# Three Q loads of a cross-covariance attention kernel issued in two parts of 68 + 60, 104 + 24 and 120 + 8 partitions

## The chip, the cores and the metric

One core of one Trainium2 chip. The metric is the time of one execution on the device in microseconds. "Before" and "after" are medians of runs. A ratio is the mean time of one kernel's fast runs over that of the other kernel's fast runs of the same rounds on the same chip, so it is not quite the ratio of the medians quoted beside it; its 95% interval stands with it. A difference in us beside a ratio is the ratio less one, times the median of before of those rounds.

The profile is that of one execution. In its lines PE is TensorE, PEld its weight loads, DVE is VectorE, ACT ScalarE, POOL GpSimd and SP SyncE; a q marks an engine's sequencer. Besides the page, the argument uses two kinds of record in the trace: the semaphore updates that the DMA engines write when their share of a transfer has landed (1552 before, 16 for each of 97 transfers), and the DMA packets, each with start, duration and size, but without the number of its engine.

## The reference

```python
Q_norm = Q / (np.linalg.norm(Q, axis=-2, keepdims=True) + 1e-10)   # Q, K, V: (8, 12, 512, 64) float32
K_norm = K / (np.linalg.norm(K, axis=-2, keepdims=True) + 1e-10)
attn = np.einsum('bhnd,bhne->bhde', Q_norm, K_norm)                # 64 x 64 for each head
attn = softmax(attn)                                               # shortened
return np.einsum('bhnd,bhde->bhne', V, attn)
```

## The kernel before

The 96 heads are 24 units of 4 heads. Each unit has three loads (Q, K, V) of 128 partitions by 4 KB, and there are 25 stores. All transfers are issued by SyncE on one queue; a planner in the kernel fixes the order of all pieces of work. At most eight transfers are in flight, as a transfer waits for the landing of the one eight places before it (in the profile, issues stand 1.27 us apart and the median from issue to landing is 10.1 us, eight times that).

```python
NB = dict(qk=6, v=5, vb=4, qkb=3, vt=3, so=10, sm=2, ab=3)       # buffers
...
def load_qk(u, x):
    if x == 0:
        qk32[u] = qp.tile([128, 2, T, D], F32, name="qk32")        # T = 16, D = 64: 4 KB for Q, 4 KB for K
    nc.sync.dma_start(out=qk32[u][:, x], in_=(Qu, Ku)[x][u * 128:(u + 1) * 128])

def store(s, i, k=None):
    rows = slice(None) if k is None else slice(k * (J // 2), (k + 1) * (J // 2))
    o = Of[s, i].rearrange("p r (j d) -> p r j d", d=D)
    nc.sync.dma_start(out=o[:, :, rows], in_=so[s, i][:, :, rows])
...
piece(("lq", u), {"DMA": X}, free, [back("lk", u, 1)], at, load_qk, u, 0)
piece(("lk", u), {"DMA": X}, free, [("lq", u)], at, load_qk, u, 1)
```

## Time and profile before

| | before |
|---|---|
| time | 132.25 us (131.68 to 132.82, 2 runs) |
| span of the profiled run | 129.8 us |
| moved | 50.66 MB, 390 GB/s over the span, 400 to 420 in the steady part |
| DMA packets under 512 B | 1552 = 97 transfers x 16 |
| 4 KB load packets | 9216, of 159 ns nearly all |

The lines behind it stand in the prediction. In the row "GB/s" each number is one of 40 slices of the span. Here the stream runs at its limit and shows as a flat row (400 to 420), so a hole in it is lost time. The row of digits above it ("DMA") tells less, as will be seen.

### The profile page before, as it was taken

What the parts mean: (1) busy time and instruction counts of PE and PEld (TensorE: products, weight loads), DVE (VectorE), ACT (ScalarE), POOL (GpSimd) and SP (SyncE); (2) the same over time, 40 slices, a digit from 0 to 9 for tenths busy, and PEclk for the clock granted to TensorE, in tenths of its full rate; (3) what the DMA queues carried; (4) which work ended last, traced back from release to release, by engine and by line L of the source; (5) the groups of instructions that cost most, each with busy time, mean ns of one, the idle gap of its engine ahead of it and who ended that gap; (6) DMA issues with size and microseconds to landing.
All of it is one profiled execution on the core that took longest, in us unless ns stands there. A gap on an engine that the chain in (4) does not pass through costs nothing.

```text
span 129.8 us, 4986 instructions
## 1 busy us (share of the span) xinstructions
PE 81.7 (63%) x2160; PEld 67.1 (52%) x2160; DVE 96.2 (74%) x161; ACT 75.2 (58%) x179; POOL 56.2 (43%) x49
## 2 busy tenths in 40 slices
PE   0045392985829835959578999479596555857610
PEld 0045381863628624749455777268374443747410
DVE  2445979999899697698999774969876778489500
ACT  0000509569566562375768569949889823795830
POOL 3000664815985308029490393371483534275000
PEclk9999999599965775556985559955999965797555
DMA  4999999999999999999999999999999999999892
GB/s 136 375 399 421 408 414 404 409 413 403 410 405 407 405 408 414 402 415 415 409 419 403 415 412 414 413 417 407 416 407 414 413 412 407 409 402 403 346 334 81
DMA packets 17190, 50.66 MB, mean 390 GB/s; under 512 B 1552, under 2 KB 2064, under 8 KB 17168
## 3 DMA queue, kind: packets, MB, share of 16 engines
q1 hardware_dynamic: 17168, 50.34, 98.1%
q8 instruction: 17, 0.28, 0.8%
q14 instruction: 5, 0.04, 0.1%
HBM read 37.75 MB, written 12.58 MB: 388 GB/s over the span
## 4 chain that ended last, share of the span: by engine, by line
DVE 34%; PE 28%; POOL 10%; ACT 9%; issue 7%; DMA 5%; SPq 1%; POOLq 0%; ACTq 0%; DVEq 0%
PE gram L196 14%; POOL r L219 9%; DVE kqs L223 8%; DVE scr L203 7%; DVE qkb L178 7%; PE po L280 6%; PE vps L265 5%; DMA qk<-in_K_dram 5%; DVE n L215 4%; DVE ab L251 4%; ACT so L154 3%; ACT vt L154 3%; PE lg L236 3%; DVE vt L156 2%; ACT ex L242 2%
## 5 line engine op out<-in xcount | busy, mean ns | idle before, releaser
L196 PE MATMUL gram<-qkb 32*128 32x128 bf16 x1536 | 37.5, 270 | 15.5 <-DVE qkb L178 10.1
L196 PEld LDWEIGHTS <-qkb 32*128 32x128 bf16 x1536 | 32.6, 121 | 19.4 <-DVE qkb L178 15.5
L158 POOL TENSOR_SCALAR vb<-v 128x1024 bf16<-128x1024 f32 x24 | 28.0, 1167 | 31.6 <-DMA v<-in_V_dram 29.0
L178 DVE CAST qkb<-qk 128x1024 bf16<-128x1024 f32 x48 | 33.2, 718 | 6.9 <-DMA qk<-in_Q_dram 5.1
L219 POOL TENSOR_TENSOR r<-n,mhalf 128x8 f32<-128x8 f32 x12 | 23.1, 1924 | 29.6 <-DVE n L215 17.3
L280 PE MATMUL po<-ab,vt 128*64 128x128 bf16 x384 | 21.5, 254 | 20.5 <-ACT vt L154 12.8
L154 ACT COPY so<-po 128x512 f32<-128x512 f32 x47 | 26.4, 591 | 11.3 <-PE po L280 11.0
L154 ACT COPY vt<-vps 128x1024 bf16<-128x1024 bf16 (+1 forms) x23 | 27.7, 1218 | 2.0 <-PE vps L265 1.8
L280 PEld LDWEIGHTS <-vt 128*64 128x64 bf16 x384 | 15.0, 127 | 26.0 <-ACT vt L154 15.4
L242 ACT ACTIVATE ex<-lg,rq 128x64 f32<-128x64 f32 x48 | 14.4, 314 | 20.9 <-PE lg L236 18.0
L203 DVE SCALAR_TENSOR_TENSOR scr<-gram,eye 64x512 f32<-64x512 f32 x24 | 16.5, 689 | 7.0 <-PE gram L196 6.7
L265 PE MATMUL vps<-identb,vb 128*128 128x128 bf16 x192 | 19.1, 262 | 0.7 <-ACT kq L154 0.7
L265 PEld LDWEIGHTS <-vb 128*128 128x128 bf16 x192 | 14.5, 118 | 3.4 <-issue 2.1
L223 DVE TENSOR_TENSOR kqs<-kq,r 64x512 f32<-64x512 f32 x8 | 11.1, 1386 | 3.7 <-POOL r L219 3.5
L251 DVE TENSOR_TENSOR ab<-ex,rinv 64x256 bf16<-64x256 f32 x24 | 10.9, 453 | 0.7
L236 PE MATMUL lg<-eye,kqs 64*128 64x64 f32 x48 | 7.0, 284 | 5.5 <-DVE kqs L223 5.1
L242 ACT ACTIVATION_READ_ACCUMULATOR ex<-lg,rq 128x1 f32 x48 | 9.8, 205 | 0.0
L236 PEld LDWEIGHTS lg<-eye,kqs 64*128 64x128 f32 x48 | 5.0, 177 | 7.8 <-DVE kqs L223 6.4
L154 ACT ACT_TABLE_LOAD x1 | 1.3, 1283 | 13.3 <-DVE scr L203 13.3
L215 DVE TENSOR_REDUCE n<-scr 128x8 f32<-128x512 f32 x12 | 8.2, 684 | 0.4
L154 ACT COPY kq<-gram 64x512 f32<-64x512 f32 x12 | 7.0, 580 | 2.0 <-DVE scr L203 1.7
L230 DVE COPY rq<-r 64x4 f32<-64x4 f32 x12 | 4.9, 411 | 2.3 <-POOL r L219 2.0
(15 smaller groups left out, 18.5 us busy)
## 6 DMA issues: line engine op xcount, KB each, us to landing
qk<-in_Q_dram SPq DMA_DIRECT2D x24, 512.0 KB, 10.1
qk<-in_K_dram SPq DMA_DIRECT2D x24, 512.0 KB, 10.2
v<-in_V_dram SPq DMA_DIRECT2D x24, 512.0 KB, 10.1
out_dram<-so SPq DMA_DIRECT2D x23, 512.0 KB, 10.0
out_dram<-so SPq DMA_DIRECT2D x2, 256.0 KB, 4.3
```

The source lines that it names most:

```text
L154: nc.scalar.copy(o, i)
L158: nc.gpsimd.tensor_scalar(out=o, in0=i, scalar1=1.0, scalar2=0.0, op0=ALU.mult, op1=ALU.add)
L178: nc.vector.tensor_copy(qkb[u][:, :, x * D:(x + 1) * D], qk32[u][:, x])
L196: nc.tensor.matmul(gram[s][:, h, r, 0], x, x, start=(t == 0), stop=(t == T - 1))
L203: nc.vector.scalar_tensor_tensor(out=scr[s][half], in0=gram[s][half, :, :, 0, half].rearrange("p h r d -> p (h r) d"), scalar=1e-20, in1=e ...
L219: nc.gpsimd.tensor_tensor(out=r8[s], in0=n2[s], in1=mhalf, op=ALU.pow)
L223: (nc.vector if eng == "DVE" else nc.gpsimd).tensor_tensor(out=kqs[s][HI], in0=kq[s][HI], in1=r8[s][HI, :, None].to_broadcast([D, 2 * HU, ...
L236: nc.tensor.transpose(l[:, h, :], kqs[s][HI, 2 * h:2 * h + 2].rearrange("p r d -> p (r d)"), eye2[HI])
L242: nc.scalar.activation(e[:, h, :], lg[s][:, h, :], AF.Exp, scale=rq[s][:, h:h + 1], accum_out=z[:, h:h + 1])
L251: nc.vector.tensor_tensor(out=a[half, :, half], in0=e[half], in1=ri[half, :, None].to_broadcast([D, HU, D]), op=ALU.mult,)
L265: nc.tensor.transpose(ps[:, n, j, :], vb[s][:, t].rearrange("p r d -> p (r d)"), identb)
L280: nc.tensor.matmul(po[s, x][e * D:(e + 1) * D, j].rearrange("p r d -> p (r d)"), w, ab[s][:, h, :])
```

## The change

The intent is to learn which engines carry a transfer that has not 128 rows. Nothing else is touched; the result stays correct.

```diff
+    CUTS = {(15, 0): 68, (18, 0): 104, (21, 0): 120}
...
-        nc.sync.dma_start(out=qk32[u][:, x], in_=(Qu, Ku)[x][u * 128:(u + 1) * 128])
+        cut = CUTS.get((u, x), 128)
+        for p0, p1 in ((0, cut), (cut, 128)):
+            if p1 > p0:
+                nc.sync.dma_start(out=qk32[u][p0:p1, x], in_=(Qu, Ku)[x][u * 128 + p0:u * 128 + p1])
```

## The prediction

In it, k is the number of engines that carry a part. Parts of 68, 60, 104, 24, 120 and 8 rows are taken to run on 4, 15, 13, 12, 15 and 8 engines; the profile after has as many semaphore updates for each. "Engines 0 to 3" is only a name for the four of the 68 rows. Its +16 rows can be worked out from these counts: with even rows, an engine that is in both parts of each cut gets 17 + 4, 8 + 2 and 8 + 1 rows in place of three times 8, so 13, 2 and 1 more. That the rows are even and that the same four engines are in all six parts is the author's estimate, as are the chances of the cases (a) to (c).

> **What bounds the kernel now.** I read the page from the top: busy times, the 40 slices, the DMA queues, then the chain that ended last, and after it SyncE's own waits and its issues in order of time, and the idle times of the second half. The page:
>
> ```profile
> span 129.8 us, 4986 instructions
> PE 81.7 (63%) x2160; PEld 67.1 (52%) x2160; DVE 96.2 (74%) x161; ACT 75.2 (58%) x179; POOL 56.2 (43%) x49
> ...
> DMA  4999999999999999999999999999999999999892
> GB/s 136 375 399 421 408 414 404 409 413 403 410 405 407 405 408 414 402 415 415 409 419 403 415 412 414 413 417 407 416 407 414 413 412 407 409 402 403 346 334 81
> DMA packets 17190, 50.66 MB, mean 390 GB/s; under 512 B 1552, under 2 KB 2064, under 8 KB 17168
> ...
> q1 hardware_dynamic: 17168, 50.34, 98.1%
> q8 instruction: 17, 0.28, 0.8%
> ...
> DVE 34%; PE 28%; POOL 10%; ACT 9%; issue 7%; DMA 5%; SPq 1%; POOLq 0%; ACTq 0%; DVEq 0%
> ```
>
> No compute engine is above 74%, while the 16 DMA engines are busy in every slice but the first and the last few and move a flat 400 to 420 GB/s. The chain gives DMA only 5% because it is followed back through DVE, PE and POOL; it does not say that the DMA has slack. The 1552 packets under 512 B are 97 transfers times 16: each transfer writes one small completion packet on every engine, so today each runs on all 16.
>
> SyncE's waits from 55 us on, and a stretch of its issues:
>
> ```profile
> SPq L173 <- ACT so L154: 10.4, 10, 2.3
> SPq L173 <- DMA out_dram<-so: 7.1, 8, 0.9
> SPq L164 <- DMA qk<-in_K_dram: 6.8, 8, 1.0
> SPq L168 <- DMA v<-in_V_dram: 6.6, 6, 2.2
> SPq L164 <- DMA qk<-in_Q_dram: 6.2, 8, 0.9
> ```
>
> ```profile
> 53.00 0.33 SPq L164 DMA_DIRECT2D qk<-in_Q_dram  x1
> 54.20 0.33 SPq L164 DMA_DIRECT2D qk<-in_K_dram  x1
> 55.49 0.40 SPq L173 DMA_DIRECT2D out_dram<-so  x1
> 56.75 0.33 SPq L168 DMA_DIRECT2D v<-in_V_dram  x1
> ```
>
> Issuing takes 0.33 us, but issues stand 1.27 us apart: before each, SyncE waits for the landing of the transfer eight places earlier. The page's median from issue to landing is 10.1 us, which is eight times 1.27. So the landings pace the kernel, and a landing is the landing of the last of 16 engines. 1.27 us for 8 rows of 4 KB on each engine is 0.159 us for a row.
>
> Landings are not even. Each completion packet's semaphore update is recorded with its time: around 63 us the 16 updates of one transfer spread over 1.9 us, around 94 us over 3.4 us, with four engines within 0.1 us of the last and the other twelve 0.9 to 3.4 us earlier. An engine loses about 1.3 us each time one of the 17 blocks of instructions (q8, 16 KB) passes over it. [...] the ninth block (69 us) sets one of the engines already late back again, so that the last update of all jumps by 1.28 us. The 17th (124.5 us) again makes one engine the straggler: in the last three stores 15 engines are done 1.1 us before it. The trace does not number the engines, so which ones carry the blocks is unknown.
>
> How close compute is behind the loads, from matching each landing with its cast: the Q load of unit 15 has 5.4 us to spare, unit 17 has 0.7, unit 20 has 0.7, unit 21 has 0.02. The waits from 60 us on agree:
>
> ```profile
> POOL r L219 <- DVE n L215: 12.8, 5, 4.0
> POOL vb L158 <- DMA v<-in_V_dram: 11.1, 7, 3.9
> ...
> DVE qkb L178 <- DMA qk<-in_Q_dram: 0.4, 1, 0.4
> ```
>
> The reader is to see that GpSimd sits waiting for V, and that DVE hardly waits for Q: it is just fed in time.
>
> [...]
>
> **The change part by part.** The schedule is made from the same plan, so the order of work on PE, DVE, ACT and GpSimd is the same; SyncE has 102 rows for 99. Three more issues of 0.33 us are 1.0 us of an engine that waits most of the time: no cost. The lanes of the eight-deep issue window shift by one, two, three: with a split inside it, the window holds half a megabyte less of eight, so some 9 us in flight instead of 10, still well over the time that an engine needs.
>
> The cost is the rows. [...]
>
> Engines 0 to 3: +16 rows, 16 x 0.159 = 2.54 us (2.07 + 0.32 + 0.16). [...] The lost time doesn't come back: in the last store the straggler works alone and still takes 0.042 us for each 1 KB row, as the engines do when all are busy; so an engine is at its own limit and does not speed up when others idle.
>
> How much reaches the end depends on where engines 0 to 3 stand in the spread.
> (a) One of them is the straggler of the end. It is busy without a gap from the first loads to its last store, so the end moves by all of it: +2.5 us. Compute allows that: Q of unit 21 lands 2.5 us later against 0.02 of slack, and [...] its K cast and all after it move by about 1.9 us (0.6 us of an existing wait for POOL is used up). The last issue moves from 124.6 to 126.5 us, within what a 2.5 us later DMA end needs.
> (b) They contain block-carrying engines, but not that one. These are some 1.1 us ahead at the end, so the DMA gives 2.5 - 1.1 = +1.4; the compute shift of up to 1.9 us, less what the shorter tail of the queue gives back, says about the same.
> (c) All four are among those that no block hits, 2.2 to 3.5 us ahead at the end: 0 to +0.4 us.
>
> Sum, with chances 0.45, 0.33 and 0.22: 0.45 x 2.5 + 0.33 x 1.4 + 0.22 x 0.2 = +1.6 us. [...]
>
> **The rivals.** First: k stays 16, rows dealt out unevenly (68 as 5 and 4). Then no engine gets more than a row or two extra, and the time stays at 132.2. For it: nothing but that no other row count was seen. I give it 0.13. Second: case (c), or slack absorbs it all, same time; against it, the slack of 0.02 and 0.7 us listed above, and that SyncE's issue follows landings. Third: 68 rows on 4 engines is slower than its rows, since four engines must carry 272 KB while the issue window stalls all others, so the starved engines add theirs: about +4 us. Against it: the early engines land 8 us after issue around 63 us and need under 3 (the first transfer's first update came 2.9 us after its issue), so their queues do not run dry over 2 us. Fourth: faster, because the engine relieved of 24 rows is the straggler. It helps only if engines 0 to 3 are all far ahead; hardly possible.
>
> **Range and chances.** 0.87 x 1.6 is +1.4; the most likely single case is +2.5, so I put the point a little above the mean: 132.25 + 1.65 = 133.9. The low end is no change (132.2), the high end is the full 2.5 on a baseline that itself ran from 131.68 to 132.82, plus some loss of order: 135.2. The line of 2% is 2.65 us, just beyond the full cost: same 0.80, slower 0.19, faster 0.01.
>
> **What would show it.** Small packets: 94 x 16 + 4 + 15 + 13 + 12 + 15 + 8 = 1571 under 512 B [...], 1600 if every part runs on 16. The updates of unit 15's Q load: 4 for the first part, the last of them 9 rows or 1.4 us later than the pace. After it the spread of the 16 updates grows by up to 2.1 us if engines 0 to 3 were late already, and shrinks if they were early: that also tells case (a) from (c). Busy times of the compute engines are unchanged within their scatter, and the idle time of GpSimd before its V casts and of DVE before its Q casts grows. The mean GB/s falls by 1 to 2%. The prediction is wrong if the count is 1571 and the time doesn't move (slack took it, or (c)), or if the time grows by over 3 us (idle engines, third rival).

## The result, and the profile after

139.31 us (139.08 and 139.53, 2 runs), ratio 1.0532 (1.0434 to 1.063): slower by 7.0 us. Both runs are in the fast state. The page after:

```profile
span 137.1 us, 4992 instructions
...
PE 82.1 (60%) x2160; PEld 67.2 (49%) x2160; DVE 95.7 (70%) x161; ACT 75.4 (55%) x179; POOL 56.0 (41%) x49
...
DMA  4999999999999999999999999999999999999982
GB/s 165 372 398 422 410 406 406 409 409 405 411 405 403 409 414 408 409 358 239 374 409 414 353 285 343 422 403 377 270 310 408 409 412 407 409 402 381 353 297 87
DMA packets 17209, 50.66 MB, mean 370 GB/s; under 512 B 1571, under 2 KB 2083, under 8 KB 17187
...
DMA 53%; PE 14%; DVE 12%; ACT 6%; issue 4%; POOL 3%; SPq 3%; DVEq 0%; POOLq 0%; ACTq 0%
```

The busy times of the compute engines are those of before. The bytes are the same. But "GB/s" has three holes, around slices 19, 24 and 29, down to 239, 285 and 270. The digits show none of it: they stay at 9, since a packet that is held up (in the holes 235 to 269 ns at the median, in place of 159) counts as busy. The chain of waits now gives DMA 53% in place of 5%.

The small packets are 1571, as the prediction's sum foretold (1600 would be 16 for every part), and the semaphore updates say the same: the six parts have 4, 15, 13, 12, 15 and 8 updates from engines, each with one more that comes some 0.5 us after the issue, whose source no run shows.

The same stretches of both kernels, in the view of busy time by stretch (stretch, its length, busy time of PE, PEld, DVE, ACT and POOL with instructions, granted clock, DMA share, GB/s). Before:

```profile
50.00:59.00 9.00, 5.81 (x115) 4.54 (x104) 7.19 (x13) 4.34 (x12) 2.97 (x3) 0.50 1.03 410
59.00:66.00 7.00, 5.19 (x186) 4.45 (x188) 5.99 (x12) 5.00 (x13) 5.09 (x5) 0.88 1.04 414
...
76.00:84.00 8.00, 6.20 (x174) 4.90 (x164) 5.61 (x11) 7.00 (x16) 3.38 (x4) 0.89 1.03 411
...
93.00:102.00 9.00, 5.64 (x196) 4.57 (x197) 6.84 (x13) 8.25 (x18) 4.46 (x5) 1.00 1.03 410
```

After:

```profile
50.00:59.00 9.00, 5.84 (x211) 4.87 (x213) 7.06 (x14) 5.78 (x15) 3.20 (x3) 0.88 1.03 409
59.00:66.00 7.00, 5.04 (x136) 4.18 (x128) 6.42 (x12) 4.28 (x13) 5.53 (x5) 0.75 1.05 286
...
76.00:84.00 8.00, 6.41 (x180) 5.30 (x180) 5.12 (x9) 5.52 (x14) 4.17 (x3) 0.79 1.02 306
...
93.00:102.00 9.00, 4.27 (x144) 3.31 (x136) 3.36 (x5) 6.21 (x9) 3.90 (x4) 0.99 1.04 305
```

The bytes missing in the three stretches, as time at the rate of before: 7 x (1 - 286/414) = 2.2, 8 x (1 - 306/411) = 2.0, 9 x (1 - 305/410) = 2.3 us, together 6.5 of the 7.0 us. So each cut costs about the same, though by the prediction the first gives four engines thirteen rows too many and the last gives them one. That already speaks against the prediction's sum.

The packets say how. Outside the holes a 4 KB load packet takes 159 ns in both kernels. In the holes most of them take over 200 ns: 88% of those that start between 60 and 66 us, 68% between 77 and 83, 72% between 94 and 101, with medians of 269, 235 and 251 ns. In the first hole that is some 270 packets, more than the 128 of the cut load, so other loads are among them. After the first 10 us, 34 were over 200 ns before, and 905 after. Added up over 159 ns and shared among 16 engines, the excess is 8.0 us after against 1.3 before: 6.7 us. Store packets (2 KB) hardly change, 84 ns for most in the holes too.

That the waits for loads grow is the consequence. Two compute groups, with their busy time, the mean of one, their idle time, and how much of it ended with a load; before, then after:

```profile
L158 POOL TENSOR_SCALAR vb<-v 128x1024 bf16<-128x1024 f32 x24 | 28.0, 1167 | 31.6 <-DMA v<-in_V_dram 29.0
L178 DVE CAST qkb<-qk 128x1024 bf16<-128x1024 f32 x48 | 33.2, 718 | 6.9 <-DMA qk<-in_Q_dram 5.1
```

```profile
L159 POOL TENSOR_SCALAR vb<-v 128x1024 bf16<-128x1024 f32 x24 | 28.3, 1183 | 45.3 <-DMA v<-in_V_dram 45.1
L182 DVE CAST qkb<-qk 128x1024 bf16<-128x1024 f32 x48 | 35.0, 751 | 16.5 <-DMA qk<-in_Q_dram 13.6
```

### The profile page after: what moved, and what is told of

Read it like the earlier page. It is cut to its first block, busy times and chain, and to the rows that moved or that the text cites. A ratio compares the mean times of both kernels' runs of the same rounds, so it can differ in the third digit from the quotient of the medians.

```text
span 137.1 us, 4992 instructions
## 1 busy us (share of the span) xinstructions
PE 82.1 (60%) x2160; PEld 67.2 (49%) x2160; DVE 95.7 (70%) x161; ACT 75.4 (55%) x179; POOL 56.0 (41%) x49
## 2 busy tenths in 40 slices
DMA packets 17209, 50.66 MB, mean 370 GB/s; under 512 B 1571, under 2 KB 2083, under 8 KB 17187
## 4 chain that ended last, share of the span: by engine, by line
DMA 53%; PE 14%; DVE 12%; ACT 6%; issue 4%; POOL 3%; SPq 3%; DVEq 0%; POOLq 0%; ACTq 0%
DMA out_dram<-so 29%; DMA qk<-in_K_dram 16%; DMA qk<-in_Q_dram 9%; PE gram L200 6%; PE po L284 4%; POOL r L223 3%; DVE scr L207 3%; DVE qkb L182 3%; ACT so L155 2%; SPq L168 2%; PE vps L269 2%; DVE kqs L227 2%; DVE ab L255 2%; ACT ex L246 2%; DVE n L219 2%
## 5 line engine op out<-in xcount | busy, mean ns | idle before, releaser
L200 PE MATMUL gram<-qkb 32*128 32x128 bf16 x1536 | 38.5, 273 | 22.6 <-DVE qkb L182 16.2
L182 DVE CAST qkb<-qk 128x1024 bf16<-128x1024 f32 x48 | 35.0, 751 | 16.5 <-DMA qk<-in_Q_dram 13.6
L223 POOL TENSOR_TENSOR r<-n,mhalf 128x8 f32<-128x8 f32 x12 | 22.5, 1876 | 23.6 <-DVE n L219 19.8
L284 PEld LDWEIGHTS <-vt 128*64 128x64 bf16 x384 | 15.5, 131 | 26.4 <-ACT vt L155 15.8
L269 PE MATMUL vps<-identb,vb 128*128 128x128 bf16 x192 | 18.4, 255 | 0.8 <-ACT kq L155 0.7
L269 PEld LDWEIGHTS <-vb 128*128 128x128 bf16 x192 | 13.9, 115 | 3.6 <-issue 2.0
L227 DVE TENSOR_TENSOR kqs<-kq,r 64x512 f32<-64x512 f32 x8 | 10.1, 1260 | 3.0 <-POOL r L223 2.8
L157 DVE COPY vt<-vps 128x512 bf16<-128x512 bf16 (+1 forms) x5 | 4.1, 840 | 1.3 <-PE vps L269 1.3
```

Source lines behind the costliest of these rows:

```text
L182: nc.vector.tensor_copy(qkb[u][:, :, x * D:(x + 1) * D], qk32[u][:, x])
L200: nc.tensor.matmul(gram[s][:, h, r, 0], x, x, start=(t == 0), stop=(t == T - 1))
L223: nc.gpsimd.tensor_tensor(out=r8[s], in0=n2[s], in1=mhalf, op=ALU.pow)
L227: (nc.vector if eng == "DVE" else nc.gpsimd).tensor_tensor(out=kqs[s][HI], in0=kq[s][HI], in1=r8[s][HI, :, None].to_broadcast([D, 2 * HU, ...
L269: nc.tensor.transpose(ps[:, n, j, :], vb[s][:, t].rearrange("p r d -> p (r d)"), identb)
L284: nc.tensor.matmul(po[s, x][e * D:(e + 1) * D, j].rearrange("p r d -> p (r d)"), w, ab[s][:, h, :])
```

## The experiments

The theories after the first look:

- *Rows* (the prediction): engines 0 to 3 get more rows, an engine is at its own limit, landings follow the slowest.
- *Window*: half-size transfers in the eight-deep window, or the issues themselves, starve the engines.
- *Crowded partitions* (new; in the expectations of the first round still "slow packets", without a place): engines that write certain partitions of SBUF at the same time hold each other up, and the parts bring this about. When it was set up it was a guess, from the 905 packets over 200 ns of the change; the added loads below test it.

### One cut at a time, and a cut along the other axis

Cuts alone: `CUTS` has only the named entry.

```diff
-    CUTS = {(15, 0): 68, (18, 0): 104, (21, 0): 120}
+    CUTS = {(15, 0): 68}          # only68; likewise only104, only120
```

> Only the 68 + 60 cut of unit 15. Rows theory (what the prediction said): 13 extra rows on engines 0 to 3, about +2.1 us over the kernel before. Slow-packet theory (while a transfer whose rows do not lie as those of a 128-row load is under way, every 4 KB load packet takes 240 to 330 ns in place of 159): about a third of the +7.1 us, +2.3 to +2.7 us. This run alone hardly parts them; its sisters do.

Measured: 134.07 us against 131.68, ratio 1.0152 (1.0085 to 1.0218), +2.0 us; 312 load packets over 200 ns.

> Only the 104 + 24 cut of unit 18. Rows theory: 2 extra rows, +0.3 us. Slow-packet theory: about +2.2 us, with one dip of the GB/s of some 6 us around 77 to 84 us and load packets of 240 to 330 ns in it, none elsewhere.

Measured: 134.45 against 131.68, ratio 1.0192 (1.012 to 1.0264), +2.5 us; 298 packets over 200 ns. One hole, at the 24th slice, and a flat row elsewhere up to the last five slices:

```profile
GB/s 143 388 407 424 407 408 404 412 406 413 404 406 402 407 413 412 408 415 412 418 403 415 393 243 361 412 409 417 411 413 412 419 414 407 404 380 322 284 249 168
DMA packets 17199, 50.66 MB, mean 381 GB/s; under 512 B 1561, under 2 KB 2073, under 8 KB 17177
```

> Only the 120 + 8 cut of unit 21. Rows theory: 1 extra row, +0.2 us. Slow-packet theory: about +2.4 us, with one dip of some 6 us around 95 us.

Measured: 133.59 against 131.68, ratio 1.0115 (1.0084 to 1.0145), +1.5 us; 252 packets over 200 ns. It is less than the +2.4 us expected, but some nine times the 0.16 us of one extra row. The three together make 6.0 us, the change 7.0 with an interval of 5.7 to 8.3.

The other axis:

```diff
-        nc.sync.dma_start(out=qk32[u][p0:p1, x], in_=...)
+        nc.sync.dma_start(out=qk32[u][:, x, t0:t1], in_=src[:, t0:t1])   # t 0 to 8, then 8 to 16
```

> The same three loads in two parts each, but cut along the free axis: two transfers of 128 partitions by 2 KB. Each part runs on 16 engines with 8 rows each, as any load of before. Window theory (the eight-deep issue window, taken up by half-size transfers, or the three extra issues themselves, starve the engines): about +7 us like the change. Slow-packet and rows theories: within 0.5 us of the kernel before, no dip, no long packets; 1600 packets under 512 B.

Measured: 132.58 against 131.68, ratio 1.0052 (1.0008 to 1.0095), +0.7 us, a little more than the 0.5 expected. 1600 small packets, 36 load packets over 200 ns, no hole. The same number of issues and the same window as the change cost a tenth of it: the window theory falls.

### Parts on all 16 engines, cut at other partitions; and stores

```diff
-    CUTS = {(15, 0): 68, (18, 0): 104, (21, 0): 120}
+    CUTS = {(15, 0): 112, (18, 0): 112, (21, 0): 112}     # cut64: 64 in place of 112
```

> Three Q loads cut 112 + 16. Both parts run on 16 engines (7 rows and 1 row), so every engine has its 8 rows as before[...]. Rows theory: no change beyond the +0.7 us that the column cut cost, 1600 small packets, no long ones. Slow-packet theory with the SBUF side as its place [...]: three dips, load packets of 240 to 330 ns, +4 to +7 us. If only engine counts that are no power of two are slow, no dip either.

Measured: 137.27 against 131.93, ratio 1.0398 (1.0324 to 1.0472), +5.2 us. 1600 small packets: all 16 engines carry both parts, 7 rows and 1 row each if the rows are even, and yet 754 load packets are over 200 ns. An odd number of engines is not needed for the loss, nor, with even rows, are more rows for some.

For 64 + 64, the figures of the crowding theory stand first:

> Three Q loads cut 64 + 64: 16 engines for each part, 4 rows each, rows even. [...] 4 KB packets of some 318 ns in three dips and +4 to +7 us. Rows theory: +0.7 us as the column cut.

Measured: 138.15 against 132.43, ratio 1.0481 (1.0416 to 1.0546), +6.4 us; 790 packets over 200 ns; of the load packets that start between 60 and 65 us, 75% are over 200 ns and the middle half takes 201 to 286. The row with the three holes:

```profile
GB/s 143 395 405 420 407 408 406 408 410 406 405 412 401 410 414 409 407 372 268 410 404 415 352 248 352 416 410 413 263 333 411 416 416 405 410 402 379 369 253 160
DMA packets 17238, 50.66 MB, mean 374 GB/s; under 512 B 1600, under 2 KB 2112, under 8 KB 17216
```

Now the same two parts of 64 partitions, but the even ones and the odd ones:

```diff
-        for p0, p1 in ((0, cut), (cut, 128)): ...
+        parts = [slice(0, 128, 2), slice(1, 128, 2)] if (u, x) in CUTS else [slice(0, 128)]
+        for p in parts:
+            nc.sync.dma_start(out=qk32[u][p, x], in_=src[p])
```

The crowding theory's figure is again the first:

> Three Q loads cut into even and odd partitions, 64 each: 16 engines, 4 rows each, as in the 64 + 64 cut[...]. [...] dips are shallower than with 64 + 64 and the time lies between: +1 to +4 us. If any load that is not 128 partitions in one piece were slow for another reason: +6 us as 64 + 64.

Measured: 132.5 against 131.83, ratio 1.0041 (1.0013 to 1.007), +0.5 us, better than expected; 34 packets over 200 ns, as before the change, and no hole:

```profile
GB/s 162 353 403 419 412 408 410 407 414 399 413 403 412 396 415 413 400 416 412 415 409 413 414 416 406 412 413 415 409 415 412 416 405 417 403 385 301 329 172 178
DMA packets 17238, 50.66 MB, mean 386 GB/s; under 512 B 1600, under 2 KB 2112, under 8 KB 17216
```

Packets (17238), bytes (50.66 MB) and engines (1600 small packets, so 16 for each part) are those of 64 + 64. What differs is which partitions a part holds and, with them, which rows of HBM it reads; the pair below takes HBM out for an added load, not for these cuts. The crowding theory still expected +1 to +4 us here, and no crowding is seen. Which engine writes which partitions of a part, no run shows. This cut and the column cut show that a load in two parts costs about 0.2 us by itself.

Cuts of three stores, loads untouched:

```diff
+        cut = {(7, 0): 68, (8, 0): 104, (9, 0): 120}.get((s, i), 128)
+        for p0, p1 in ((0, cut), (cut, 128)): ...
+                nc.sync.dma_start(out=o[p0:p1, :, rows], in_=so[s, i][p0:p1, :, rows])
```

> The kernel before with three stores (not loads) cut 68 + 60, 104 + 24 and 120 + 8. Theory that the crowded place is SBUF's write side or HBM's read side: no dips, store packets stay at 84 ns, the time grows by rows alone (up to +2.5 us, likely +1 to +2). Theory that any odd engine count slows the engines[...]: +5 to +7 us with three dips.

Measured: 132.84 against 131.93, ratio 1.0029 (0.9993 to 1.0065): +0.4 us, not clear of nothing. 33 load packets over 200 ns, 105 of 5888 store packets over 110 ns (30 before). So reading SBUF by these odd cuts is no trouble that can be measured. The parts have the rows of the change, and they cost less than the rows theory wanted. (Stores cut 64 + 64 were not run.)

### The partitions written, and the rows, each by itself

To the kernel before, one load is added ahead of unit 15 into a spare tile that nobody reads: 32 KB for each of a few partitions, one packet for each partition, from the same HBM addresses.

```diff
+        if (u, x) == (15, 0):
+            nc.sync.dma_start(out=extra[slice(0, 4)],   # near; apart: slice(0, 16, 4); two: slice(0, 2), ...
+                              in_=Qu[0:32].rearrange("(p r) d -> p (r d)", r=8))
```

The expectations were recorded in three rounds (first 0 to 3 and four apart, then two and 32 apart, then three), so the later ones know the earlier results. For partitions 0 to 3 and for those 4 apart, the crowding theory's figures stand first. For 0 and 1, the first figures hold if the two slow all engines, the second if they slow only themselves; for 0 to 2 it is the other way round. For those 32 apart, the first hold if they crowd, the second if only neighbours do.

> The kernel before with one added load ahead of unit 15: 4 rows of 32 KB into partitions 0 to 3 of a spare tile (4 engines, as much for each of them as 8 rows of 4 KB). [...] +2.5 to +4 us, and the last of the 4 landings some 3 to 5 us after the pace. Rows theory: +1.3 us at most, like its sister. HBM-side theory: like its sister.

> The same added load, the same bytes from the same addresses [...], but into partitions 0, 4, 8 and 12. [...] no long packets: only the load of engines 0 to 3, +1.27 us if one of them is the straggler of the end, less if not. HBM-side theory: the same as its sister with partitions 0 to 3.

> As the added load into partitions 0 to 3, but 2 rows of 32 KB into partitions 0 and 1: 2 engines[...]. [...] while the two run together, all 4 KB packets take about 2 x 159 = 318 ns, for about 2 us; +0.5 to +1.2 us. [...] packets of the other 14 stay at 159 ns.

> As the added loads into partitions 0 and 1 and into 0 to 3, with 3 rows of 32 KB into partitions 0 to 2[...]. With two, the packets of the other engines stayed at 159 ns, with four all went to some 700. [...] others at 159 ns, under +0.7 us. [...] most 4 KB packets at 300 to 500 ns for 1 to 2 us, +0.7 to +1.5 us.

> The added load of 4 rows of 32 KB into partitions 0, 32, 64 and 96. [...] packets of 318 ns or more for 2 us or so, +0.5 to +1.5 us. [...] no long packets, like partitions 0, 4, 8 and 12.

Measured (the packets of the added load; what most 4 KB packets of all other traffic took while the added packets overlapped; how many 4 KB packets of the run after its first 10 us were over 200 ns):

| partitions | added packets, us | other 4 KB packets, ns | over 200 ns | ratio |
|---|---|---|---|---|
| 0, 4, 8, 12 | 1.21, 1.21, 1.21, 1.21 | 159 | 27 | 1.0012 (0.9976 to 1.0048) |
| 0, 1 | 1.21, 1.84 | 159, but 8 of 296 to 348 | 40 | 1.0024 (0.9992 to 1.0055) |
| 0, 1, 2 | 2.40, 2.39, 3.08 | 195 to 210 | 121 | 1.0021 (0.9983 to 1.0059) |
| 0, 1, 2, 3 | 2.10, 2.36, 3.57, 3.73 | 570 to 710 | 127 | 1.0127 (1.0057 to 1.0197) |
| 0, 32, 64, 96 | 1.21, 1.90, 2.00, 2.70 | 280 to 440 | 135 | 1.0119 (1.0072 to 1.0166) |

The profiled run of partitions 0 and 1 fell in the slow state (clock 0.751); its packets are read for what stands beside them, not for its span. Its ratio is from fast runs.

The same in the stretch from 60 to 62 us: partitions 0, 4, 8, 12, then 0 to 3.

```profile
60.00:62.00 2.00, 2.00 (x106) 1.83 (x96) 1.58 (x3) 0.34 (x2) 1.91 (x2) 0.93 0.99 407
```

```profile
60.00:62.00 2.00, 1.90 (x56) 1.57 (x45) 1.50 (x3) 1.13 (x8) 0.69 (x1) 1.00 1.07 179
```

What follows:

- Same bytes, same HBM addresses, same number of packets, and the rate of the whole core is 407 in one case and 179 GB/s in the other. Only the partitions written differ, so the cause lies in where the load is written in SBUF. For this load an HBM cause is out.
- Four partitions apart, each 32 KB packet takes 1.213 us, 27.0 GB/s, and disturbs no one: the others stay at 159 ns. Neighbouring partitions crowd (up to 1.84 us for 0 and 1, 3.73 for 0 to 3), and so do 0, 32, 64 and 96 (up to 2.70 us). With these the other packets took 280 to 440 ns, where 0 and 1 left them at 159; why, no run shows.
- With partitions 0 and 1, one of the two packets takes 1.84 us in place of 1.21; 8 of the 4 KB packets then take 296 to 348 ns, about twice 159, few enough to be those of one or two engines; all others go on at 159. So my theory that all engines go at the pace of the most crowded partitions fell: with two there is no such effect, with three the others slow by a quarter (195 to 210 ns), with four about fourfold (570 to 710). Why the step from two to four is so steep stays open.
- Three neighbouring partitions were expected to cost 0.7 us or more if they held up all; they held up all, mildly, and the time did not grow measurably (ratio 1.0021, 0.9983 to 1.0059).

At last the prediction's own sum, without crowding: four added loads into partitions 4 apart are to give each of four engines thirteen, two and one rows more at units 15, 18 and 21. Whether these are the engines of the change's parts, and the same in all four loads, no run shows.

```diff
+        EXTRA = {(15, 0): (0, 7), (15, 1): (1, 6), (18, 0): (2, 2), (21, 0): (3, 1)}     # first partition, rows
+        if (u, x) in EXTRA:
+            p, r = EXTRA[u, x]
+            nc.sync.dma_start(out=extra[p:16:4, :r * T * D], in_=Qu[0:4 * r].rearrange("(p r) d -> p (r d)", r=r))
```

> The rows of the prediction alone, without crowding: the kernel before with added loads that give engines 0 to 3 (4 rows in partitions 4 apart) what the change gave them: 13 rows of 4 KB each at unit 15 (as 7 and 6), 2 at unit 18, 1 at unit 21. No long packets. Prediction's case (a): +2.5 us; case (b): +1.4. From the landings of the run with partitions 0, 4, 8 and 12, where the latest of these four engines stood 0.75 us ahead of the last one: 2.5 - 0.75 or less, and by compute's slack less again: +0.5 to +1.5 us.

Measured: 132.07 against 132.43, ratio 0.9985 (0.9955 to 1.0016): no cost that can be measured, less than the +0.5 expected. 36 packets over 200 ns.

The trace of this run shows a delay all the same. From unit 15 on, the last of the 16 updates of a load comes up to 1.9 us later than the other 15, so one engine did fall behind. The last Q load lands at 106.25 us (104.67 in the profile of before), the last copy into a store tile ends at 125.88 (124.58), but the span ends at 130.3 (129.8). The last stores wait for their copies; the other engines run out of work, and the late one catches up: it is 1.3 us behind in the store issued at 121.80 and 0.4 us in the last, where before one engine was 1.1 us behind. So the delay reached the last copies and mostly not the end.

The run with partitions 0, 4, 8 and 12 tells where the four engines stood there. The V load just ahead of the added one has its 16 updates from 59.80 to 61.95 us. The four updates of the added load come at 61.05, 61.06, 61.76 and 62.45; less its 1.21 us, if an engine goes on to the added load right after V, its engines had finished with V at 59.84, 59.85, 60.55 and 61.24: 2.1, 2.1, 1.4 and 0.7 us ahead of the last one. In that run the stragglers are others. In the run of the added rows it was otherwise: the four updates of the first added load come at 60.75, 60.81, 61.53 and 63.42; less the 1.06 us of its 28 KB, the fourth had finished with V at 62.36, and the last of all updates of that V load is at 62.35. There one of the four was the straggler.

## Why the prediction was wrong

The prediction said 133.9 us (132.2 to 135.2) and "within 2%" at 0.80; it came out at 139.3. By its own steps:

- *Landings pace the kernel, compute is just behind*: right. GpSimd and DVE wait longer for V and Q, their busy times are unchanged, and the loss in the holes goes nearly whole into the time (6.5 of 7.0 us).
- *94 x 16 + 4 + 15 + 13 + 12 + 15 + 8 = 1571 small packets*: right, and the updates of each part are as many. That the same four engines are in all six parts, no run shows, as the trace does not number them.
- *"Engines 0 to 3: +16 rows, 16 x 0.159 = 2.54 us"*: this step failed, twice over. It priced a row at 0.159 us wherever it is written. That price held here only where partitions did not crowd (159 ns with partitions 4 apart, 570 to 710 with 0 to 3). While a part is under way, most 4 KB packets take over 200 ns (medians 235 to 269 in the three holes), and the excess over all packets, 6.7 us for each engine, is the cost. That the partitions written decide it is shown for the added loads; for the parts it is argued from the same long packets. I had taken the straggler's unchanged 0.042 us per 1 KB row, in a store and alone, as proof that nothing is shared; it says nothing about writing loads into SBUF (in the holes store packets stay at 84 ns while load packets grow).
- *The extra rows reach the end in case (a) by 2.5 us, (b) by 1.4, (c) by 0 to 0.4*: this step failed too. The rows alone cost nothing measurable (0.9985, 0.9955 to 1.0016), and not because of case (c): in the trace of that run one of the four engines was the last one, and the spread of the 16 updates grew from 2.7 us to 4.5 around unit 15, which is the prediction's own sign of case (a). "The end moves by all of it" was wrong: the last copies came 1.3 us later, not 1.9, and at the last stores, which wait for these copies, the late engine caught up. In another run the four stood 0.7 to 2.1 us ahead, so where the four stand changes from run to run.
- *Third rival, about +4 us, engines starved while four carry 272 KB*: the nearest in size, for a reason that isn't it. 112 + 16, with 16 engines for each part, costs 5.2 us, and its trace shows 754 long packets and a DMA share of 1.04 in its first hole (296 GB/s), not idle engines. That its figure came nearest is luck.
- *"The mean GB/s falls by 1 to 2%"*: it fell from 390 to 370, 5%.

What the rivals lacked was a cause that slows most load packets, whatever the rows. The long packets and the lost time agree over the runs (time from the ratio; excess of the 4 KB packets of the profiled run over 159 ns per engine, less that of before, 1.28 us):

| run | time, us | excess, us |
|---|---|---|
| the change | +7.0 | 6.7 |
| only 68 + 60 | +2.0 | 1.7 |
| only 104 + 24 | +2.5 | 2.0 |
| only 120 + 8 | +1.5 | 1.5 |
| 112 + 16, three times | +5.2 | 5.6 |
| 64 + 64, three times | +6.4 | 5.9 |
| even and odd, three times | +0.5 | 0.0 |
| columns, three times | +0.7 | 0.0 |

Still open: how the rows of a part are dealt to its engines (and so why 120 + 8, one row off, has 252 long packets where 68 + 60 has 312); why even and odd halves show no crowding at all; whether HBM has a share in the cost of the block cuts, whose parts also read other rows of HBM; why 0, 32, 64 and 96 slow the others; and the steep step from two to four neighbouring partitions.

## What to carry to other kernels

Load 128 partitions in one piece, or cut along the free axis (0.2 us a cut here); if a load must be cut by partitions, take every second one, not a block: two blocks of 64 cost 2.1 us a cut here, even and odd halves 0.2. A load into a few neighbouring partitions can slow the loads of the other engines too (195 to 210 ns a packet with partitions 0 to 2, 570 to 710 with 0 to 3, in place of 159), so a small odd transfer in the middle of a saturated stream is not priced by its own bytes. Look for it in the GB/s row and in packet durations, since the busy share stays full while packets are held up; and before pricing uneven rows, find out whether the engines that get them are the late ones, and whether the end waits for them.
